# Block 2's attention with the low part of k on both halves of the partitions

## The chip, the cores and the metric

The kernel runs on one core of one Trainium2 chip. The metric is the device time of one execution in microseconds; the median of three runs is given, and the lowest and the highest beside it. A profile of one execution was recorded apart from these; all rows come from it. The engines are TensorE (PE for its matmuls, PEld for its weight loads), VectorE (DVE), ScalarE (ACT), GpSimd (POOL) and SyncE (SP, whose queue issues the loads).

## What is computed

Two blocks over 256 tokens of width 1024, all in float32. Block 1 is an attention and a gated delta rule side by side, then a mixture of 32 experts. Block 2 takes its result as the latent tokens, and 256 context tokens, modulates both, projects q (latent only), k and v, and runs two attentions beside each other, of 8 heads of 64 each, over the latent and the context keys together: type a with 2 heads of k and v, a window of 128 tokens and a sink, type b with 8 heads and a 2D neighbourhood with a bias table. Then an output projection and a gated FFN of 2816 columns follow. The part that matters, of type a; type b has its own k and v for each head and adds the bias to the local scores:

```python
def _window_gqa_latent(q, k, v, k_ctx, v_ctx, sink):
    ...
    s_loc = jnp.einsum('bnqkgd,bnjkd->bnkgqj', qb, kb).astype(jnp.float32) * scale
    s_loc = jnp.where(mask, s_loc, -jnp.inf)
    s_ctx = jnp.einsum('bnqkgd,bjkd->bnkgqj', qb, k_ctx).astype(jnp.float32) * scale
    ...
    p = jax.nn.softmax(jnp.concatenate([s_loc, s_ctx, sink_col], axis=-1), axis=-1)
```

## The kernel before

Every matrix product is made of parts. A float32 operand is split into a high part that TensorE's reduced format holds exactly (a ScalarE copy, split_w's line L185 for weights) and a low part, the rest (a subtraction on VectorE or POOL, L192). A projection or FFN product is three matmuls, high by high, low by high and high by low (mm3, recorded at the helper's line L99, as all matmuls are; transposes stand at L102).

**Scores of block 2.** A head has 64 channels, half of the 128 partitions. So q lies with its high part on one half of the partitions and its low part on the other (qa and qb, made in qk_heads, L1128 to L1153). The high part of k lies on both halves (kAa, kAb), so that one matmul over all 128 rows gives both q_high k_high and q_low k_high. The low part of k lies on one half only: kLa for type a holds the two heads of k, kLb for type b the two heads of a pair on the two halves. The product with it is a second matmul, over 64 rows, with q's high part. All four live in one tile per side, k, made by kv_tiles (L1159): for the latent it is a slot of the ring (k0, L1407), for the context it lies in the pool kvc (L1264 to L1269), where kAb has a tile of its own.

In scores (L1526) a unit is a type, a pair of heads m and a half qt of the queries; it makes eight products into two PSUM tiles (the context's first, then the latent's), adds the mask (type a, L1541) or the bias (type b, L1543) by one more matmul each, takes the maximum (L1545, VectorE), the exponential (L1555, ScalarE) and the scaling by one over the sum (L1564 ScalarE, L1566 VectorE). turn (L1569) transposes the probabilities on TensorE and copies them out, outputs (L1581) multiplies by v. There are 16 units, type a first; the loop (L1613 to L1648) puts a unit's scores one ahead of the transposes of the unit before (AHEAD = 1):

```python
                kh, kl = (kAa[s][:, m // 2], kLa[s][rs, m // 2]) if typ == 0 else (kAb[s][:, s_, m], kLb[s][rs, m])
                PE.matmul(scs[s_][:, s], lhsT=q[:, s_, m, ts], rhs=kh, start=True, stop=False)
                PE.matmul(scs[s_][:, s], lhsT=q[rs, s_, m, ts], rhs=kl, start=False, stop=s == 1)
```

**What sets the order.** A scheduler places the recorded instructions on each engine once, when the program is built; on the chip each engine takes its own in that order and waits by semaphores. Weights pass through a ring of nine tiles of 128 x 2048 (load_block, L164, ring_tile, L1165); a load is issued on SP's queue when the slot's last reader is done. During attention some ring slots are held by k0 and the bias tables; cst3 (the rotary table, the neighbourhood mask and a reversal matrix), the rotary factors rgt (rg in the trace) and the latent's v (vb0) have places in the stage's own pool.

**The FFN** (L1682 to L1748) takes 11 blocks of 256 hidden columns. Block 0's gate weights are split early (w0, L1685). mod_T (L1385) makes the transposed and modulated x in eight steps, hif (high, ScalarE) and lof (low, VectorE). g2B (L1691), the last gate spread over the rows, is laid into the place of vb0. ffn_up(b) (L1699) loads and splits gate and up weights and makes pfg and pfu, 48 products each; fsg (L1720) is the SiLU. The low part of block 0's up weights is computed on POOL.

Of the kernel before, what the change touches and what calls it, by code (L numbers as in the profile page):

```python
# [9 lines left out]
F32 = mybir.dt.float32  # L10
# [12 lines left out]
# columns of the shape-only constant array  # L23
C_ID, C_TRI = 0, 128
C_IO = 256                     # 1..32 along the free axis
C_DN = C_IO + 32               # 8..1
C_SP = C_DN + 8                # p % 32 + 1
C_BM = C_SP + 1                # [p, 4]: p // 32 == j
C_SL = C_BM + 4                # rows of a modulation chunk's partial sums: latent, context
C_LT = C_SL + 2                # [i, j] of 8 by 8: j < i  # L30
C_W = C_LT + 64
# columns of the one of block 2's attention
C_ROPE = 0                     # [p, 2 token tiles, cos 64 | signed sin 64]
C_CM = C_ROPE + 256            # [p, 64]: NEG where the column lies outside row 63 - p % 64's neighbourhood
C_J = C_CM + 64                # reversal of each half's 64 rows, times the root of the head's size
# [3 lines left out]
def constants():  # L39
    """arrays that depend on the shapes alone"""  # L40
# [31 lines left out]
    # [e, unit, slot]: e == 4 * unit + slot // 32  # L72
# [4 lines left out]
class Ordered:  # L77
    """the tensor engine; between start() and stop() it takes its instructions in the program's order"""
# [27 lines left out]
def tile_kernel(ctx: ExitStack, tc: tile.TileContext, I, out, dbg=None):  # L106
# [9 lines left out]
    def open_stage(name, psum, base=False):  # L116
        """the pools of one stage; psum: banks per tag"""
        st = ExitStack()
        if base:
            S_["base"] = st.enter_context(tc.tile_pool(name="base_" + name, bufs=1, reuse_waits="tile"))  # L120
        S_["act"] = st.enter_context(tc.tile_pool(name="act_" + name, bufs=1, reuse_waits="tile"))
        if psum:
            S_["ps"] = st.enter_context(tc.tile_pool(name="ps_" + name, bufs=1, space=PSUM, reuse_waits="tile"))
        S_["banks"] = psum
        S_["tmp"] = S_["act"]
        S_["junk"] = {"a": ("zg", 2), "c": ("jk", 1), "d": ("prb2", NPR)}[name]
        return st
# [4 lines left out]
    def open_part(name, psum):  # L132
        """pools of a part of the stage: SBUF for what only the part needs, and all of its PSUM"""
# [22 lines left out]
    # ---------------------------------------------------------------- helpers  # L156
    def load_block(src, name, extra=None):
        """src: DRAM AP [128, a, b] with a * b = 2048; extra: a pool and its slots that the stage adds to the ring"""
# [8 lines left out]
    def cols(w, c0, n=256):  # L167
        """columns c0:c0+n of a [1024, *] matrix, contraction row d = p * 8 + k"""
        return w[:, c0:c0 + n].rearrange("(p k) c -> p k c", k=8)

    def rows(w, r0):
        """rows r0:r0+256 of a [*, 1024] matrix, contraction row k * 128 + p"""
# [28 lines left out]
    def after(ins, first):  # L201
        """ins behind first in their engine's order"""
# [6 lines left out]
    def bcast_dma(dst, src, n):  # L209
        """n elements of DRAM copied to all partitions"""  # L210
        SP.dma_start(dst, bass.AP(tensor=src.tensor, offset=src.offset, ap=[[0, P], [1, n]]))

    def rstd_of(ssq, n, mean, eps, name):
        """(ssq * mean + eps) ** -0.5 over [128, n]"""
# [6 lines left out]
    def row_ssq(src, name, col=None):  # L221
        """src [128, 2, 1024] -> sums of squares [128, 2]"""
# [9 lines left out]
    def row_rstd(src, name):  # L232
        """src [128, 2, 1024] -> rstd [128, 2]"""
        return rstd_of(row_ssq(src, name), 2, 1.0 / D, EPS, name)

    def diags(r, name):
        """diagonal matrices of the two columns of r [128, 2]"""
# [5 lines left out]
    def norm_rows(src, name):  # L243
        """the rows' rstd, a column for each token tile"""
# [3 lines left out]
    def pairs_T(src, dg, tags, by_pair=False):  # L248
        """four PSUM tiles of pairs of k, [128 d, 2, 256 t]: see scaled_T"""
# [10 lines left out]
    def scaled_T(src, dg, tags, by_pair=False):  # L260
        """yields k, PSUM [128 d, 256 t] of src[t, p * 8 + k], times r[t] where dg = diags(r);
        tags: the banks of the four pairs of k, each open until its pair was taken"""
# [3 lines left out]
    # -------------------------------------------------------------- constants  # L266
# [13 lines left out]
    cols_ = const.tile([P, 4, 8], F32)    # gains down the partitions: attn_norm, ffn_norm, norm1_g, norm2_g  # L280
    gA, gF, gN1, gN2 = (cols_[:, i] for i in range(4))
    lvl = ab([P, 5, 32], "lvl", "lvl", dt=BF16)     # masks of the doubling

    mqk = ring.tile([P, 2048], F32, tag="blk", name="mqk")
    POOL.memset(mqk[:, :P], 0.0)                 # takes its slot of the ring
# [21 lines left out]
    maskn = const.tile([P, P], BF16)      # [j, i]: NEG where j > i  # L307
    maskc = const.tile([P, P], BF16)      # [i, j]: NEG where j > i

    # ============================================================ block 1: norm  # L310
# [33 lines left out]
    PE.transpose(pm, tri, ident)          # [i, j]: j <= i  # L344
# [15 lines left out]
    # ------------------------------------------------- modulations of block 2  # L360
# [4 lines left out]
    DVE.tensor_tensor(sc2t, sc2t, c2t, op=ALU.mult)                         # silu  # L365
    sil = ep.tile([P, 8, 2, 16], F32, tag="sil", name="sil")
    POOL.tensor_copy(sil, bc(sc2t.rearrange("p a k -> p k a"), 16))
    mod = pers.tile([P, 6, 8, 2], F32, tag="mod", name="mod")     # [p, vector, k, latent / context], d = p * 8 + k
    w_mod = I["w_mod_2"][0]

    def mod_steps():
        """a vector's quarters by column groups: column 8 c + k of group j is d = (32 j + c) * 8 + k, and blocks of 32
        by 32, transposed, bring its two sides to mod's places"""
# [35 lines left out]
    # ------------------------------------------------------ GDN q, k, v with conv  # L409
    gT = {}  # L410

    def proj_T(c0, name, sink):
        """columns c0:c0+256 in two [128 ch, 256 t] PSUM tiles, each given to sink with its place; a step at a time"""
# [21 lines left out]
    def gdn_proj(kind, base):  # L435
        def conv(c, pp_):
# [11 lines left out]
            DVE.scalar_tensor_tensor(o, th, 1.0, a, op0=ALU.add, op1=ALU.mult)   # 2 * silu  # L448
# [17 lines left out]
    # ------------------------------------------------------------- gates  # L466
# [17 lines left out]
    DVE.scalar_tensor_tensor(ny, y, -1.0, y, op0=ALU.mult, op1=ALU.min)     # -|y|  # L484
# [9 lines left out]
    DVE.scalar_tensor_tensor(pp, pp, 1.0, s, op0=ALU.add, op1=ALU.mult)     # log1p(z) / 2  # L494
    DVE.tensor_scalar(y, y, 0.0, None, op0=ALU.max)
    DVE.scalar_tensor_tensor(gg, pp, 2.0, y, op0=ALU.mult, op1=ALU.add)     # softplus
    DVE.scalar_tensor_tensor(gg, gg, -1.0, expA[:, None, :].to_broadcast([P, 2, 4]), op0=ALU.mult, op1=ALU.mult)
    DVE.tensor_scalar(bt, bt, 1.0, None, op0=ALU.add)
    DVE.reciprocal(bt, bt)                                                   # beta
    dump("gg", gg)  # L500
    # running sums of the log decay inside each half, and the sums after a token of the first half
    pall = aa([P, P], "kn", "pall", bufs=2)
    DVE.tensor_scalar(pall, tri, -1.0, 1.0, op0=ALU.mult, op1=ALU.add)       # [j', j]: j' > j
# [3 lines left out]
    nG = aa([P, 3, 4], "nG", "nG")        # -G0, -G1, suffix sums  # L507
# [3 lines left out]
    # ------------------------------------------------------------ gz, MoBA q, k, v  # L511
    def proj_tok(c0, name, sink):
        """columns c0:c0+256 in a [128 t, 2, 256] PSUM tile"""
# [15 lines left out]
    def projections():  # L529
        """of v, the gate and MoBA, a step at a time"""  # L530
# [64 lines left out]
    BD = []                                  # B's blocks of 32 on the diagonal, transposed  # L595
# [9 lines left out]
    # ------------------------------------- (I + B)^-1 of each half, block sizes doubling  # L605
    # up to 32: T, and its transpose W, hold the blocks on the diagonal side by side
# [32 lines left out]
    def level_32(blk):  # L639
        """pairs of blocks of 32: all of W's, the first of T's"""  # L640
# [84 lines left out]
    # the output's norm: o = c * ob with c = rq / (2 * sqrt(128))  # L725
# [30 lines left out]
    mst = at([P, 4, 3, 2, 2], "mst", "mst")          # [.., m, (max, sum, 1 / sum), head, q tile]  # L756
# [59 lines left out]
    def moba_out(m, s_, pe_, pT):  # L816
        rs = slice(64 * s_, 64 * s_ + 64)
        vs = slice((2 * m + s_) * 64, (2 * m + s_) * 64 + 64)
        # transposed blocks: (k0, q0), (k0, q1), (k1, q1)
# [32 lines left out]
    # ============================================================ block 1: experts  # L852
# [51 lines left out]
    def first_max(v, n, dn, name):  # L904
        """max over the last axis and the one-hot of its first place"""
# [19 lines left out]
    # rank of every expert in the group: those of larger logits, and those of the same logit before it  # L925
# [20 lines left out]
    rrp = at([P, 2, 32], "rrp", "rrp")              # place in the expert's list + 1, 0 where not selected  # L946
    DVE.scalar_tensor_tensor(rrp, prk, 1.0, sel, op0=ALU.add, op1=ALU.mult)
    # pairs past the 32 places of an expert, and how many there are
# [3 lines left out]
    # one-hots of the places of units 2 * g and 2 * g + 1  # L952
# [16 lines left out]
    oh = sm([P, 2, 2, 8], "oh")                     # one-hots of the first and second place  # L969
# [6 lines left out]
    # the two shares 1 / (1 + e2), e2 / (1 + e2), times the group's probability  # L976
# [18 lines left out]
    # weights and norm factors of the pairs  # L995
# [5 lines left out]
    # ------------------------------------------------------------ the experts  # L1001

    wg_, wu_, wd_ = I["w_gate"][0], I["w_up"][0], I["w_down"][0]
    # the slots of the experts' weights in the order in which they come free; None: the ring's
# [3 lines left out]
    def ring_slot():  # L1008
        """takes one of the ring's slots out of the experts' order"""
        queue.remove("r")  # L1010

    def wexp(w, u, part, name):
        """a quarter of the weights of a unit's four experts, [128, expert, 512]: two contraction rows
        p * 8 + k of a gate or up matrix; the row p * 2 + part % 2 of a down matrix, one half of its columns"""
# [23 lines left out]
    def gather(u):  # L1038
        """the rows of x of a unit, [128 d, 8 k, 128 places], times the norm's gain"""
# [20 lines left out]
    def weights(g):  # L1060
        """weight and norm of every place of units 2 * g and 2 * g + 1, one column per unit"""
# [766 lines left out]
```

## Time and profile before

| | us |
|---|---|
| median of three runs | 882.71 |
| lowest, highest | 881.35, 885.22 |
| span of the profiled execution, first to last instruction | 879.8 |
| TensorE busy | 825.3 (94%) |
| VectorE busy | 422.3 (48%) |
| ScalarE busy | 296.3 (34%) |
| POOL busy | 105.6 (12%) |

The profiled execution has no time of its own beside its span. A stretch's busy times are the sums of its instructions; on TensorE neighbours overlap, so that the distance between two starts, and not a matmul's duration, tells what one costs. PEclk is the clock granted to TensorE as a share of full speed, 2.4 GHz; 0.50 is the lower level, 1.2 GHz. A timeline's row joins instructions of one line and the same operands, xcount of them; its first time is the first one's start, its second reaches to the last one's end. In brackets stands how long the engine was idle before, and what it waited for.

### The profile page before, as it was taken

To read this page: it belongs to the slowest core of one execution; us is meant where nothing else is said; L and a number is where in the kernel's file an instruction comes from. 1 tells how busy PE (TensorE), PEld (TensorE's weight loads), DVE (VectorE), ACT (ScalarE), POOL (GpSimd) and SP (SyncE) were. 2 spreads that over 40 slices of the span, in tenths; PEclk is the share of its full clock that TensorE was granted. 3 is DMA by queue.
4 is the path that set the end of the run, shared out by engine and by line. 5 is a ranking of instruction groups with operands and counts; after the bars stand their busy time and mean duration, and the time that the engine had idled before them with its cause. 6 is when DMAs were issued, how large, how long until landed. Compare 5 with 4: busy or idle time off the path is not lost.

```text
span 879.8 us, 15327 instructions
## 1 busy us (share of the span) xinstructions
PE 825.3 (94%) x6436; PEld 667.5 (76%) x6436; DVE 422.3 (48%) x927; ACT 296.3 (34%) x523; POOL 105.6 (12%) x90
## 2 busy tenths in 40 slices
PE   9999999999789988996998997999997999999997
PEld 8887887867656645773865897667686999999996
DVE  4866454644322111323224788555664655545555
ACT  4542143433110000101004662456643444444332
POOL 3111000332000000000000577100022100000000
PEclk9999999999889999897999999589999999999999
DMA  7999787495799999999599135010271655555101
GB/s 218 353 386 391 264 296 281 133 385 171 280 386 386 387 387 387 378 382 376 208 386 333 48 53 164 1 48 2 96 239 48 202 187 187 192 191 187 54 1 48
DMA packets 123416, 200.18 MB, mean 228 GB/s; under 512 B 15481, under 2 KB 62001, under 8 KB 123345
## 3 DMA queue, kind: packets, MB, share of 16 engines
q1 hardware_dynamic: 123152, 199.08, 64.5%
q8 instruction: 51, 0.84, 0.4%
q0 software_dynamic: 192, 0.11, 0.1%
q14 instruction: 21, 0.16, 0.1%
HBM read 198.23 MB, written 1.05 MB: 226 GB/s over the span
## 4 chain that ended last, share of the span: by engine, by line
PE 47%; DVE 4%; POOL 4%; issue 3%; DMA 2%; ACT 1%; SPq 1%; DVEq 0%; POOLq 0%; ACTq 0%
PE pfg L99 7%; PE pfu L99 7%; PE pf L99 7%; PE sc L99 6%; PE pgat L99 3%; PE pgu L99 2%; PE po L99 2%; PE ptp L102 2%; POOL latl L192 2%; PE pyd L99 2%; DMA eg<-in_w_gate_dram 1%; PE ckbp L99 1%; PE pqa L99 1%; PE pqb L99 1%; POOL rq L218 1%
## 5 line engine op out<-in xcount | busy, mean ns | idle before, releaser
L99 PEld LDWEIGHTS pgat<-S,x 128*128 128x128 f32 x256 | 62.5, 335 | 3.7 <-DVE xg L1051 2.1
L99 PE MATMUL pgat<-S,x 128*128 128x128 f32 x256 | 63.0, 404 | 0.6 <-PEq L1200 0.5
L99 PE MATMUL pfu<-lof,fuh 128*128 128x256 f32 x176 | 50.2, 285 | 0.0
L99 PE MATMUL pfu<-hif,fuh 128*128 128x256 f32 x176 | 50.2, 285 | 0.0
L99 PE MATMUL pfu<-hif,ful 128*128 128x256 f32 x176 | 50.2, 285 | 0.0
L99 PE MATMUL pfg<-hif,fgl 128*128 128x256 f32 x160 | 45.3, 283 | 0.0
L99 PE MATMUL pfg<-lof,fgh 128*128 128x256 f32 x160 | 45.2, 283 | 0.0
L99 PE MATMUL pfg<-hif,fgh 128*128 128x256 f32 x160 | 45.2, 283 | 0.0
L192 DVE TENSOR_TENSOR fdl<-fd,fdh 128x512 fp32r<-128x512 f32 x44 | 27.5, 687 | 31.0 <-ACT fdh L185 31.0
L1051 DVE TENSOR_TENSOR xg<-pgat,cols__83 128x512 f32<-128x512 f32 x15 | 10.4, 692 | 63.7 <-PE pgat L99 63.7
L99 PE MATMUL pyd<-ed,hid 128*32 128x512 f32 x256 | 34.1, 664 | 3.8 <-ACT hid L1326 3.8
L1320 ACT ACTIVATE sg<-pgu,r1s 128x256 f32<-128x256 f32 x8 | 3.8, 474 | 96.7 <-PE pgu L99 73.9
L1545 DVE TENSOR_REDUCE st<-sc 128x1 f32<-128x512 f32 x32 | 21.9, 691 | 28.6 <-PE sc L99 28.3
L185 ACT ACTIVATE fdh<-fd 128x1024 fp32r<-128x1024 f32 x22 | 22.1, 1052 | 39.0 <-issue 39.0
L99 PE MATMUL pf<-fdl,fh 128*128 128x512 f32 x88 | 35.0, 398 | 0.0
L99 PE MATMUL pf<-fdh,fh 128*128 128x512 f32 x88 | 34.7, 394 | 0.0
L99 PE MATMUL pf<-fdh,fl 128*128 128x512 f32 x88 | 34.1, 393 | 0.0
L99 PEld LDWEIGHTS pfu<-hif,fuh 128*128 128x128 f32 x176 | 34.1, 194 | 0.0
L99 PEld LDWEIGHTS pfu<-hif,ful 128*128 128x128 f32 x176 | 34.1, 193 | 0.0
L99 PEld LDWEIGHTS pfu<-lof,fuh 128*128 128x128 f32 x176 | 34.0, 193 | 0.0
L185 ACT ACTIVATE fuh<-fu 128x1024 fp32r<-128x1024 f32 x22 | 22.1, 1052 | 31.2 <-issue 28.7
L99 PE MATMUL sc<-k,qa 128*128 128x256 f32 (+1 forms) x64 | 28.1, 501 | 3.7 <-DVE qa L1149 3.5
(691 smaller groups left out, 2209.6 us busy)
## 6 DMA issues: line engine op xcount, KB each, us to landing
eg<-in_w_gate_dram SPq DMA_DIRECT2D x32, 1024.0 KB, 14.1
eu<-in_w_up_dram SPq DMA_DIRECT2D x32, 1024.0 KB, 14.1
ed<-in_w_down_dram SPq DMA_DIRECT2D x32, 1024.0 KB, 14.1
wmod<-in_w_mod_dram SPq DMA_DIRECT2D x24, 1024.0 KB, 9.5
fg<-in_w_gate_dram SPq DMA_DIRECT2D x11, 1024.0 KB, 5.4
fu<-in_w_up_dram SPq DMA_DIRECT2D x11, 1024.0 KB, 5.3
fd<-in_w_down_dram SPq DMA_DIRECT2D x11, 1024.0 KB, 5.0
kv<-in_w_in_dram SPq DMA_DIRECT2D x5, 1024.0 KB, 13.9
```

What stands on the lines that cost most here:

```text
L99: return self._keep(self.engine.matmul(*args, **kwargs))
L102: return self._keep(self.engine.transpose(*args, **kwargs))
L185: S_["hi"] = ACT.activation(hf[:, s], vf[:, s], AF.Copy)
L192: i = (POOL if c in pool else DVE).tensor_tensor(lf[:, s], vf[:, s], hf[:, s], op=ALU.subtract)
L218: S_["pow"] = POOL.tensor_tensor(r, v, mhalf[:, :n], op=ALU.pow)
L1051: DVE.tensor_tensor(xg[:, ks], p, bc(gF[:, ks], P), op=ALU.mult)
L1320: ACT.activation(sg, pgu[:, 0], AF.Silu, scale=r1s[:, u:u + 1])
L1545: DVE.tensor_reduce(t_[:, 0, s_:s_ + 1], sc, axis=AX.XY, op=ALU.max)
```

## The change

qk_heads writes the low part of k by heads, as the high part, and copies it to the other half of the partitions as well: two more VectorE copies of 64 x 512 for each half of the heads and each side, eight in all. With both low parts there, every second score product reads all 128 rows of q, so that it also adds the product of the two low parts. The two kLb need twice their room: the context's is a tile of its own, the latent's takes the place of the transposed context (hcT), and the tile k is half as large, so that the latent's leaves the ring. In exchange cst3, rgt and vb0 move into one ring tile, mixed, and in the FFN g2B takes a ring slot. The core of the diff:

```diff
@@ qk_heads @@
-            lo = q[there, i, ms] if s is None else kLb[s][here, ms]
+            lo = q[there, i, ms] if s is None else kLb[s][here, i, ms]
...
                 DVE.tensor_copy(hi[there, i, ms], hi[here, i, ms])
+                DVE.tensor_copy(kLb[s][there, i, ms], kLb[s][here, i, ms])
@@ kv_tiles @@
-        k = make([P, 8, 256], f"k{s}", F32R)
-        kAa[s], kLa[s], kLb[s] = k[:, 0:2], k[:, 2:4], k[:, 4:8]
+        k = make([P, 4, 256], f"k{s}", F32R)
+        kAa[s], kLa[s] = k[:, 0:2], k[:, 2:4]
@@ the context's tiles @@
-            kAb[1] = kvc.tile([P, 2, 4, 256], F32R, tag="kAb1", name="kAb1")
+            kAb[1], kLb[1] = (kvc.tile([P, 2, 4, 256], F32R, tag=nm, name=nm) for nm in ("kAb1", "kLb1"))
@@ block 2 @@
-    cst3 = at([P, C_W3], "cst3", "cst3")
+    mixed = ring_tile("mixed", F32)
+    vb0 = mixed[:, 0:1024].rearrange("p (a b) -> p a b", a=2)
+    rgt = mixed[:, 1024:1536].rearrange("p (i t s c) -> p i t s c", i=2, t=2, s=2)
+    cst3 = mixed[:, 1536:1536 + C_W3]
     SP.dma_start(cst3, I["cst3"])
...
-    k0 = ring_tile("k0").rearrange("p (a b) -> p a b", a=8)
...
+    kLb[0] = kvc.tile([P, 2, 4, 256], F32R, tag="hcT", name="kLb0")
...
-    rgt = at([P, 2, 2, 2, 64], "rg", "rg")
@@ scores @@
-                rs = (TOP, BOT)[s_]
-                kh, kl = (kAa[s][:, m // 2], kLa[s][rs, m // 2]) if typ == 0 else (kAb[s][:, s_, m], kLb[s][rs, m])
+                kh, kl = (kAa[s][:, m // 2], kLa[s][:, m // 2]) if typ == 0 else (kAb[s][:, s_, m], kLb[s][:, s_, m])
                 PE.matmul(scs[s_][:, s], lhsT=q[:, s_, m, ts], rhs=kh, start=True, stop=False)
-                PE.matmul(scs[s_][:, s], lhsT=q[rs, s_, m, ts], rhs=kl, start=False, stop=s == 1)
+                PE.matmul(scs[s_][:, s], lhsT=q[:, s_, m, ts], rhs=kl, start=False, stop=s == 1)
@@ FFN @@
-        g2B = row_bc(mod[:, 5, :, 0], at([P, D], "vb0", "g2B"), ("mo", "sm"))
+        g2B = row_bc(mod[:, 5, :, 0], ring_tile("g2B", F32)[:, 0:D], ("mo", "sm"))
```

After the change the lines of this part stand two or three lower.

With the tiles the order moves at three places. The first is VectorE in the latent projections, where k's high part (kAb) and low part (k before, kLb now) are laid down; latl is the low part of the next weights, rqv the step that POOL's rq, and with it the normalization qn of the next heads, waits for. Before:

```order
L1153 COPY kAb_4443<-kAb_4443 64x512
L192 TENSOR_TENSOR latl<-lat,lath 128x512 x2
L1087 TENSOR_REDUCE hss<-hsq 128x8
L1153 COPY kAb_4443<-kAb_4443 64x512
L216 TENSOR_SCALAR rqv<-hss 128x8
L1151 SCALAR_TENSOR_TENSOR k_4324<-pqk,gcol,kAb_4443 64x512 x2
L1153 COPY kAb_4443<-kAb_4443 64x512
L1089 TENSOR_TENSOR qn__4796<-lqp,rq 128x512
```

and now:

```order
L1153 COPY kAb_4447<-kAb_4447 64x512
L192 TENSOR_TENSOR latl<-lat,lath 128x512
L1154 COPY kLb_4408<-kLb_4408 64x512 x2
L192 TENSOR_TENSOR latl<-lat,lath 128x512
L1087 TENSOR_REDUCE hss<-hsq 128x8
L1153 COPY kAb_4447<-kAb_4447 64x512
L1151 SCALAR_TENSOR_TENSOR kLb_4408<-pqk,gcol,kAb_4447 64x512 x2
L1153 COPY kAb_4447<-kAb_4447 64x512
L216 TENSOR_SCALAR rqv<-hss 128x8
L1154 COPY kLb_4408<-kLb_4408 64x512 x2
```

Two pairs of copies have come in, and rqv stands behind the two splits of k, where it stood ahead of them.

The second place is ScalarE at the start of the FFN, where fuh is the high part of an up block, fgh that of a gate block, and the first fsg the SiLU of block 0. Before:

```order
L228 ACTIVATE jk_6161,rfq<-x 128x1024
L185 ACTIVATE fuh<-fu 128x1024 x2
L185 ACTIVATE fgh<-fg 128x1024 x2
L1401 ACTIVATE hif<-mt,mod 128x256 x8
L1455 ACTIVATE g2B<-prb 128x4x128 x2
L1720 ACTIVATE fsg<-pfg 128x512
L185 ACTIVATE fuh<-fu 128x1024 x2
```

and now:

```order
L228 ACTIVATE jk_6169,rfq<-x 128x1024
L1404 ACTIVATE hif<-mt,mod 128x256 x8
L1458 ACTIVATE g2B<-prb 128x4x128 x2
L1722 ACTIVATE fsg<-pfg 128x512
L185 ACTIVATE fuh<-fu 128x1024 x2
L185 ACTIVATE fgh<-fg 128x1024 x2
L185 ACTIVATE fuh<-fu 128x1024 x2
```

The splits of block 0's up weights and of block 1's gate weights, which stood ahead of hif, stand behind fsg.

The third is TensorE at the same point. Before, the products with block 0's gate and up weights are woven together:

```order
L99 MATMUL pfg<-hif,fg0h 128x256
L99 MATMUL pfu<-hif,fuh 128x256
L99 MATMUL pfg<-lof,fg0h 128x256
L99 MATMUL pfg<-hif,fg0l 128x256
L99 MATMUL pfg<-hif,fg0h 128x256
L99 MATMUL pfu<-lof,fuh 128x256
L99 MATMUL pfu<-hif,ful 128x256
L99 MATMUL pfu<-hif,fuh 128x256
```

and now:

```order
L99 MATMUL pfg<-hif,fg0h 128x256
L99 MATMUL pfg<-lof,fg0h 128x256
L99 MATMUL pfg<-hif,fg0l 128x256
L99 MATMUL pfg<-hif,fg0h 128x256
L99 MATMUL pfg<-lof,fg0h 128x256
```

Only pfg stands there, 48 products of it; pfu(0) follows behind them, woven with pfg(1).

## Rows read from the trace of the kernel before

**Rows 1.** The page, part 1: span, and busy time, share and instructions of TensorE.

```profile
span 879.8 us, 15327 instructions
PE 825.3 (94%) x6436; PEld 667.5 (76%) x6436; DVE 422.3 (48%) x927; ACT 296.3 (34%) x523; POOL 105.6 (12%) x90
```

**Rows 2.** Windows: length; busy us of PE, PEld, DVE, ACT, POOL; PEclk; DMA; GB/s.

```profile
549.84:589.84 40.00, 39.87 (x171) 25.84 (x171) 22.77 (x60) 19.98 (x50) 2.43 (x3) 0.66 0.00 1
589.84:638.04 48.20, 47.80 (x305) 33.78 (x306) 28.60 (x71) 30.40 (x64) 0.71 (x1) 1.00 0.20 66
549.84:576.70 26.86, 26.73 (x82) 16.81 (x82) 14.47 (x38) 12.22 (x31) 2.43 (x3) 0.50 0.00 1
600.00:610.00 10.00, 9.60 (x75) 7.42 (x74) 4.23 (x11) 4.67 (x8) 0.00 (x0) 1.00 0.01 2
```

**Rows 3.** Timeline, PE, type a (start, us, instruction, idle before): half clock, then full.

```profile
549.84 2.11 PE L99 MATMUL sc<-k,qa 128*128 128x256 f32 x4 [3.54 <-DVE qa L1149]
551.88 0.29 PE L99 MATMUL sc<-maskc,identb 128*128 128x128 bf16 x1
...
581.86 1.31 PE L99 MATMUL sc<-k,qa 128*128 128x256 f32 x4
583.10 0.23 PE L99 MATMUL sc<-maskc,identb 128*128 128x128 bf16 x1
```

**Rows 4.** Timeline, PE, one head of type b.

```profile
590.25 0.36 PE L99 MATMUL sc<-kAb,qb 128*128 128x256 f32 x1
...
591.48 0.70 PE L99 MATMUL sc<-bias,cst 128*128 128x256 f32 x2
```

**Rows 5.** Timeline, PE, two heads near 578 us, and narrow windows inside them.

```profile
577.29 2.04 PE L99 MATMUL sc<-k,qa 128*128 128x256 f32 x8
...
577.90 0.51 PE L99 MATMUL sc<-k,qa 128*128 128x256 f32 x2
...
578.33 0.38 PE L99 MATMUL sc<-k,qa 64*128 64x256 f32 x2
```

**Rows 6.** Timeline, PE, FFN: two neighbours at full clock, two at half.

```profile
697.70 0.28 PE L99 MATMUL pfg<-lof,fgh 128*128 128x256 f32 x1
697.82 0.29 PE L99 MATMUL pfg<-hif,fgl 128*128 128x256 f32 x1
...
686.16 0.42 PE L99 MATMUL pfu<-hif,ful 128*128 128x256 f32 x1
686.38 0.42 PE L99 MATMUL pfu<-hif,fuh 128*128 128x256 f32 x1
```

**Rows 7.** Timeline, DVE, latent projections.

```profile
522.93 0.43 DVE L1153 CAST kAb<-kAb 64x512 fp32r<-64x512 f32 x1
...
529.31 0.69 DVE L1089 TENSOR_TENSOR qn__4872<-lqp,rq 128x512 f32<-128x512 f32 x1 [1.75 <-POOL rq L218]
...
549.10 1.41 DVE L1149 TENSOR_TENSOR qa<-pqk,qa 64x512 fp32r<-64x512 f32 x2
```

**Rows 8.** Timelines of PE, ACT, POOL and DVE at the start of the FFN.

```profile
684.04 0.39 PE L99 MATMUL pfg<-lof,fg0h 128*128 128x256 f32 x1 [1.14 <-DVE lof L1402]
...
703.34 0.28 PE L99 MATMUL pfu<-hif,fuh 128*128 128x256 f32 x1
...
689.40 2.23 ACT L1455 ACTIVATE g2B<-prb 128x512 f32<-128x512 f32 x2
694.66 0.60 ACT L1720 ACTIVATE fsg<-pfg 128x512 f32<-128x512 f32 x1 [3.02 <-PE pfg L99]
697.80 2.01 ACT L185 ACTIVATE fuh<-fu 128x1024 fp32r<-128x1024 f32 x2 [2.54 <-PE pfu L99]
...
679.97 5.16 POOL L192 TENSOR_TENSOR ful<-fu,fuh 128x512 fp32r<-128x512 f32 x4
...
682.44 2.96 DVE L1402 SCALAR_TENSOR_TENSOR lof<-mt,mod,hif 128x256 fp32r<-128x256 f32 x2
685.73 0.47 DVE L1402 SCALAR_TENSOR_TENSOR lof<-mt,mod,hif 128x256 fp32r<-128x256 f32 x1
```

More of the change, by code (lines that the diff above doesn't have):

```diff
@@ L1406, in tile_kernel @@
         kvw[c0] = load_block(cols(w_in2, c0), "lat")
-    k0 = ring_tile("k0").rearrange("p (a b) -> p a b", a=8)
-    hth, htl = mod_T(xf, [ss[:, 4, i:i + 1] for i in range(2)], mod[:, 1], mod[:, 0], "l", lambda: kv_tiles(0, lambda shape, nm, dt: k0 if nm == "k0" else at(shape, nm, nm, dt=dt)))
+    hth, htl = mod_T(xf, [ss[:, 4, i:i + 1] for i in range(2)], mod[:, 1], mod[:, 0], "l",
+                     lambda: kv_tiles(0, lambda shape, nm, dt: vb0 if nm == "vb0" else at(shape, nm, nm, dt=dt)))
     S_["cxt"] = "tr"
     next(ctxh)
+    kLb[0] = kvc.tile([P, 2, 4, 256], F32R, tag="hcT", name="kLb0")
     if CXB:
```

## The prediction

> **What bounds the kernel now.** I read the page first, then windows over block 2's attention, then TensorE's timeline inside it, then the two places that the change also moves: the latent projections on VectorE and the start of the FFN. TensorE is busy for 94% of the 879.8 us span [rows 1], and the windows say that attention is no exception: from the first score product at 549.84 to the end of the last at 638.04 the engine has work all the time, 39.87 of 40.00 us in the heads of type a and 47.80 of 48.20 us in those of type b, while VectorE works 22.77 and 28.60 us and ScalarE 19.98 and 30.40 us [rows 2]. So what leaves TensorE here leaves the path, until VectorE is met. The granted clock stands at half (the lower level, 1.2 GHz) from the start until about 576.7 us [rows 2]; before it fell, TensorE had waited 3.54 us for the last split of q [rows 3].
>
> Busy does not mean dense. In type b one head's four products, high and low, context and latent, begin at 590.25 and its bias product at 591.48: 1.23 us, 0.31 us a product [rows 4]. In the FFN products of 256 columns over 128 rows begin 0.12 us apart at full clock and 0.21 at half [rows 6]. In type a four products take 2.04 us at half clock and 1.24 at full [rows 3]. The span of this execution is 2.9 us under the median of the three runs, 882.71; I add that at the end.
>
> **The products.** Before, every second product of a head is over 64 rows, and each neighbour is over 128. The change keeps their number, 128, their columns and very nearly their order, and gives all of them 128 rows. What will such a product cost? The nearest in form is the FFN's, 0.12 us, hundreds in a row. Inside attention there is one place where the order puts two 128-row products side by side: the second's end makes the pair 0.51 us long where one takes 0.38 to 0.39, and by their own lengths they begin 0.12 to 0.22 us apart, not 0.31 [rows 5]. So the dear step is the change between the two heights. I take 0.12 (0.21 at half clock), since after the change the whole group is of one form as in the FFN, and keep 0.22 as the dear end.
>
> - Type b, 16 heads at full clock: 1.23 - 4 x 0.12 = 0.75 us each, 12.0.
> - Type a, four heads at full clock: 1.24 - 0.48 = 0.76 each, 3.0; two heads, placed with two equal products side by side, took 1.98 us together (8 products, 2.04 to the end of the last's tail) [rows 5]; they give back 1.0.
> - Type a, ten heads at half clock: 2.04 - 4 x 0.21 = 1.20 each, 12.0.
>
> That is 28.0. Could more come off, because the clock returns sooner with denser work? In type a hardly: 40.0 - (12.0 + 3.0 + 1.0) = 24.0 us are left for TensorE, and VectorE has 22.8 us of work in it [rows 2], so at most 1.2 more, 29.2 in all. That nearness also costs. A head passes from TensorE to VectorE (the maximum), ScalarE (the exponential), back for the transposes and on; only one unit is scored ahead. Before, the slow products of 32 heads covered these turns, with 4% idle in the worst ten microseconds [rows 2]; 4% of the 60 us that remain is 2.4, which I take off: **25.6 gained**. At the dear price of 0.22 the heads give 16 x 0.35 + 4 x 0.36 + 10 x (2.04 - 4 x 0.4) and the two nothing, 11.4, the poor end.
>
> A page speaks against the change here. The Trainium skill, TensorE: Matmul & The Clock Gate, "Why this matters for your kernels", says that one product with few contraction rows takes as long as one with 128, and that products in different row groups run side by side, so that small ones are best kept small and laid in different groups. The trace bears out the second half: two 64-row products, one of each half, stand in one 0.38 us entry [rows 5]. By the first half the time between products would not come from the height, nothing would be gained, and the sum would be that of the third rival below; the 0.31 against 0.12 of rows 4 and 6 is why I go by the trace.
>
> **The copies.** qk_heads now also copies the low part of k to the other half: eight more VectorE instructions of 64x512. The nearest row is the high part's copy, 0.43 us [rows 7]. Four are the context's and stand in the expert stage, long before; VectorE is busy for 48% of the span [rows 1], and I count them as hidden in its idle time there; if that cover were gone they would cost 1.7. Four are the latent's and stand some 25 us before the first score, in the VectorE chain whose end, the split qa at 549.10 [rows 7], releases it: 1.72 us at most in themselves. That chain has waits for POOL's powers, such as 1.75 us [rows 7], and a copy that falls into one is free; the order puts one pair behind the step that POOL waits for. One step of that kind (rqv) also moves behind a split, which could add a turn on POOL of about the same size, so the ends are 0 and 3.4; I take **0.9 lost**. The half-clock stretch begins after this wait as before.
>
> **The start of the FFN.** The second block of weights, fu(0), now gets the ring slot that attention's high part of the latent k held, and its split on ScalarE stands behind fsg, which needs all 48 products pfg(0). TensorE therefore has no pfu(0) to weave in and all of pfg(0) goes first. Before, TensorE reaches the first pfu(1) at 703.34, with 144 products behind it; it waited for lof, 1.14 us at one place [rows 8]. After: g2B ends at 689.40 + 2.23 = 691.63, by when the 48 products are through; fsg adds 0.60; the first half of fuh, 1.0 (half of 2.01) [rows 8], is there at 693.2. The 96 products left take 96 x 0.12 = 11.5: 704.7. POOL's ful follows fuh by 5.16 / 4 = 1.29 [rows 8], in which products are missing: 706.0, 2.7 later than before. TensorE's idle time of some 2 us would let the clock fall, and the last such stretch, 15 products at 0.21, cost 1.4. On the other side ful is gone from the time of lof, which took 1.48 us each beside it and 0.47 alone [rows 8]: up to 2.0 back. Between 0.7 (lof earlier, no clock loss) and 7.5 (ful now slows the four splits fgl by the same 1 us each and the clock falls) I take **3.0 lost**. What is late next is fgh(1), two splits behind fuh on ScalarE.
>
> **Moves without a price.** cst3, the rotary table and the latent v share one ring tile, and its load goes ahead of three weight loads on SP's queue; those are delayed by one small load, and each is used 10 us or more after it lands. g2B's ring slot and fu(0)'s are free well before their use, as attention ends over 40 us earlier; if that cover went, the load would show as a DMA wait ahead of fuh.
>
> **The sum.** -25.6 + 0.9 + 3.0 = -21.7: a span of 858.1, and with the 2.9 of the median **861.0 us**. Good end: -29.2 + 0 + 0.7 = -28.5, 854; poor end of the one price: -11.4 + 3.4 + 7.5 = -0.5, which needs all three at once.
>
> **Rivals.** First, the chain VectorE, ScalarE, TensorE becomes the bound in attention. For it: 22.8 of VectorE's us against 24.0 left on TensorE in type a, and one unit of lead only; against it: in type b the rest, 48.2 - 12.0 = 36.2, stays 6 us above ScalarE. If type a gives 7 instead of 16 and type b 6 instead of 12, or if products come 0.22 apart, some 13 are gained: -13 + 4 = -9, 873.7. Second, the clock stays at half until the end of attention, because shorter products leave more waits. The page's clock row came back at 576.7 with the old, thinner work, which is against it. Type b's 36.2 us would take about 1.65 times that (2.04 to 1.24 for the same products [rows 3]), 60 instead of 48: -16 + 12 + 4 = 0, 882.7. Third, the other side: the height of a product does not set its time, the 0.31 us comes from the operands of the attention (weights new for each product). Then the copies and the FFN's start are all that is left: 1.7 + 4.2 = +5.9, 888.6; it decides as soon as attention gains less than the copies and the FFN's start cost. By the page named above this is how it would come out; rows 5, with equal neighbours inside attention closer than unequal ones, is against it.
>
> **Chances.** Forecast 0.76, first rival 0.15, second 0.04, third 0.05. The range must leave out no more than 2 in 10: it reaches from 853, the good end with a little for the clock, to 873, which takes in half of the first rival. Half a per cent, 4.4 us, is about what can be told from no change: the forecast and the first rival are faster, 0.91; the second is the same, 0.04; the third slower, 0.05.
>
> **What would show it.** In the profile after: all score products 128*128 and 0.12 apart, a head's four in 0.48 (right) or still 1.23 (third rival); attention 62 to 64 us long, TensorE under 100% busy in type a with VectorE above 85%; the half clock over before half of type a has passed, and none in type b; first scores 0 to 2 us later in relation to the projections; on ScalarE fsg before the first fuh, with a hole on TensorE between pfg(0) and pfu(0) of about 2 us, and the first pfu(1) some 24 us after the first pfg instead of 20.9. The prediction is wrong if TensorE's idle time in attention is above 10 us, or if the FFN's start costs more than 8.

## The result and the profile after

The changed kernel takes 858.26 us (median of four runs, 857.41 to 859.44) beside 882.39 before (four runs, one more than the three above): a ratio of 0.9724, 95% interval 0.9703 to 0.9744. All ratios below are to the kernel before, measured beside it, with their 95% intervals. The forecast was 861.0, in a range of 853 to 873. The span fell from 879.8 to 856.1 us; part 1 of the page after:

```profile
span 856.1 us, 15332 instructions
PE 796.8 (93%) x6436; PEld 656.8 (77%) x6436; DVE 425.2 (50%) x935; ACT 294.4 (34%) x523; POOL 106.7 (12%) x90
```

TensorE makes as many instructions as in [rows 1] and is busy 28.5 us less; VectorE has eight more, the copies. TensorE's timeline after, one head of type b, stands against [rows 4]:

```profile
574.62 0.39 PE L99 MATMUL sc<-kAb,qb 128*128 128x256 f32 x1
574.85 0.28 PE L99 MATMUL sc<-kLb,qb 128*128 128x256 f32 x1
574.97 0.28 PE L99 MATMUL sc<-kAb,qb 128*128 128x256 f32 x1
575.08 0.28 PE L99 MATMUL sc<-kLb,qb 128*128 128x256 f32 x1
575.20 0.59 PE L99 MATMUL sc<-bias,mixed 128*128 128x256 f32 x2
```

All four products read 128 rows. The first step is 0.23 us, the others 0.12: 0.58 from the first product to the bias, where it was 1.23. Type a, first and later, stands against [rows 3]:

```profile
551.29 1.22 PE L99 MATMUL sc<-k,qa 128*128 128x256 f32 x4 [3.55 <-DVE qa L1149]
552.32 0.33 PE L99 MATMUL sc<-maskc,identb 128*128 128x128 bf16 x1
...
557.77 0.74 PE L99 MATMUL sc<-k,qa 128*128 128x256 f32 x4 [1.10 <-ACT prb L1557]
...
562.34 0.72 PE L99 MATMUL sc<-k,qa 128*128 128x256 f32 x4
562.90 0.23 PE L99 MATMUL sc<-maskc,identb 128*128 128x128 bf16 x1
```

Four products take 1.03 us at half clock (551.29 to 552.32) and 0.56 at full. The wait for qa ahead of the first is as long as before, and a new kind of wait appears, for the exponential prb. The windows (type a, type b, the stretch at half clock) stand against [rows 2]:

```profile
551.29:574.62 23.33, 21.44 (x174) 18.97 (x174) 21.44 (x60) 17.60 (x47) 2.46 (x3) 0.87 0.02 4
574.62:610.36 35.74, 35.34 (x303) 29.50 (x300) 28.41 (x71) 30.13 (x65) 0.71 (x1) 1.00 0.17 59
551.29:557.40 6.11, 5.38 (x24) 4.82 (x24) 4.90 (x9) 1.64 (x3) 2.46 (x3) 0.50 0.00 0
```

The 88.2 us of attention have become 59.1, from 551.29 to 610.36. In type a TensorE and VectorE are now equally busy, 21.44 of 23.33 us each, and TensorE has 1.9 us of idle time; the clock is back at 557.4 instead of 576.7. The latent projections stand against [rows 7]; VectorE's timeline shows the new copies, which a trace calls casts:

```profile
520.41 0.88 DVE L1154 CAST kLb<-kLb 64x512 fp32r<-64x512 f32 x2
...
526.19 0.87 DVE L1154 CAST kLb<-kLb 64x512 fp32r<-64x512 f32 x2
...
550.55 1.41 DVE L1149 TENSOR_TENSOR qa<-pqk,qa 64x512 fp32r<-64x512 f32 x2
```

0.44 us each, as taken. And the start of the FFN (PE, then ACT, POOL, DVE), against [rows 8]:

```profile
655.01 0.38 PE L99 MATMUL pfg<-hif,fg0h 128*128 128x256 f32 x1
...
663.67 0.28 PE L99 MATMUL pfg<-hif,fg0l 128*128 128x256 f32 x1
665.58 0.39 PE L99 MATMUL pfu<-hif,fuh 128*128 128x256 f32 x1 [1.63 <-ACT fuh L185]
...
666.93 0.58 PE L99 MATMUL pfu<-hif,ful 128*128 128x256 f32 x1 [0.85 <-POOL ful L192]
...
679.65 0.28 PE L99 MATMUL pfu<-hif,fuh 128*128 128x256 f32 x1
...
663.98 0.60 ACT L1722 ACTIVATE fsg<-pfg 128x512 f32<-128x512 f32 x1 [1.94 <-PE pfg L99]
664.47 2.00 ACT L185 ACTIVATE fuh<-fu 128x1024 fp32r<-128x1024 f32 x2
...
665.60 5.92 POOL L192 TENSOR_TENSOR ful<-fu,fuh 128x512 fp32r<-128x512 f32 x4 [13.26 <-ACT fuh L185]
...
667.44 5.22 DVE L192 TENSOR_TENSOR fgl<-fg,fgh 128x512 fp32r<-128x512 f32 x4 [6.93 <-ACT fgh L185]
```

TensorE finishes pfg(0), waits 1.63 us for fuh, which stands behind fsg, and 0.85 for ful; the first pfu(1) comes at 679.65, 24.6 us after the first pfg, where it came 20.9 us after it. Beside each other, POOL's ful and VectorE's fgl take 1.48 and 1.3 us each. Before, ful took 1.29 [rows 8] and fgl 0.62:

```profile
689.93 2.49 DVE L192 TENSOR_TENSOR fgl<-fg,fgh 128x512 fp32r<-128x512 f32 x4
```

The balance of the two profiles:

| | before | after | difference |
|---|---|---|---|
| first score product | 549.84 | 551.29 | +1.45 |
| first score to the end of the last | 88.20 | 59.07 | -29.13 |
| from there to the first pfg | 44.36 | 44.65 | +0.29 |
| first pfg to first pfu(1) | 20.94 | 24.64 | +3.70 |
| rest | 176.5 | 176.5 | 0.0 |
| span | 879.8 | 856.1 | -23.7 |

Not all of the first line is the copies': a step of the expert stage ahead of the first copy, va of the context, begins at 384.35 before and at 385.00 after. That 0.65 is one execution against another; in the profiles below the first score comes between 549.9 and 555.4 us, with copies and without, and stages are compared from their own starts.

### The profile page after: what moved, and what is told of

It reads as the page before. It is cut to its first block, busy times and chain, and to the rows that moved or that the text cites. A ratio compares the mean times of both kernels' runs of the same rounds, so it can differ in the third digit from the quotient of the medians.

```text
span 856.1 us, 15332 instructions
## 1 busy us (share of the span) xinstructions
PE 796.8 (93%) x6436; PEld 656.8 (77%) x6436; DVE 425.2 (50%) x935; ACT 294.4 (34%) x523; POOL 106.7 (12%) x90
## 4 chain that ended last, share of the span: by engine, by line
PE 45%; DVE 7%; POOL 3%; ACT 2%; issue 2%; DMA 1%; SPq 0%; DVEq 0%; POOLq 0%; ACTq 0%
PE pfu L99 8%; PE pfg L99 7%; PE pf L99 7%; PE sc L99 3%; PE pgat L99 3%; PE pgu L99 3%; PE po L99 2%; PE ptp L102 2%; PE pyd L99 2%; PE ckbp L99 2%; PE pqa L99 1%; PE pqb L99 1%; POOL latl L192 1%; DMA sinkB<-in_sink_a_dram 1%; PE pt L99 1%
## 5 line engine op out<-in xcount | busy, mean ns | idle before, releaser
L185 ACT ACTIVATE fdh<-fd 128x1024 fp32r<-128x1024 f32 x22 | 22.1, 1052 | 36.9 <-issue 36.9
L185 ACT ACTIVATE fuh<-fu 128x1024 fp32r<-128x1024 f32 x22 | 22.1, 1053 | 36.4 <-issue 28.6
L192 DVE TENSOR_TENSOR fgl<-fg,fgh 128x512 fp32r<-128x512 f32 x40 | 27.7, 754 | 9.3 <-ACT fgh L185 9.3
L99 PE MATMUL pgu<-eg,xg 128*32 128x256 f32 x512 | 31.5, 387 | 0.0
```

The lines of the kernel that those rows point to most:

```text
L99: return self._keep(self.engine.matmul(*args, **kwargs))
L185: S_["hi"] = ACT.activation(hf[:, s], vf[:, s], AF.Copy)
L192: i = (POOL if c in pool else DVE).tensor_tensor(lf[:, s], vf[:, s], hf[:, s], op=ALU.subtract)
```

## The experiments

The theory: a product costs 0.12 us where its neighbour has the same number of rows, and some 0.19 more where it has not; the rest of the change only costs. The rivals: the 64-row product is dear by itself; the gain is the clock's; the moved tiles gain something.

**Products back to 64 rows (e_half).**

```diff
-                kh, kl = (kAa[s][:, m // 2], kLa[s][:, m // 2]) if typ == 0 else (kAb[s][:, s_, m], kLb[s][:, s_, m])
+                rs = (TOP, BOT)[s_]
+                kh, kl = (kAa[s][:, m // 2], kLa[s][rs, m // 2]) if typ == 0 else (kAb[s][:, s_, m], kLb[s][rs, s_, m])
...
-                PE.matmul(scs[s_][:, s], lhsT=q[:, s_, m, ts], rhs=kl, start=False, stop=s == 1)
+                PE.matmul(scs[s_][:, s], lhsT=q[rs, s_, m, ts], rhs=kl, start=False, stop=s == 1)
```

> The change with the second product of every head put back to 64 rows; copies, tiles and the FFN's order stay as in the change. My theory (a change of height between neighbouring products costs time, the rest of the change only costs): attention as long as before, 88 us from the first score product to the end of the last, products 0.31 us apart in type b, half clock again for some 27 us; the copies' 0.8 us and the FFN start's 3.7 us remain, so 882.4 + 4.5 = 887 us. Rival (the gain comes from the new places of the tiles, not from the products): 858 to 865. Rival (copies and FFN start cost nothing that counts): 882.

Measured: 899.42 us (888.36 to 902.14), ratio 1.0138 (1.0087 to 1.0189), slower than before by 1 to 2%, and 12 us above the 887 expected. The 0.31 us spacing is back:

```profile
597.71 0.36 PE L99 MATMUL sc<-kAb,qb 128*128 128x256 f32 x1
598.00 0.38 PE L99 MATMUL sc<-kLb,qb 64*128 64x256 f32 x1
598.31 0.39 PE L99 MATMUL sc<-kAb,qb 128*128 128x256 f32 x1
```

So the tiles and copies gain nothing. Nine of the ten runs fall into two groups, three around 888.5 (near the 887 expected) and six around 900, with mean granted clocks of 0.953 to 0.955 and 0.937 to 0.945. The profiled run, 893.3, lies between: its clock is 0.955, and its first score comes at 555.44, 5.6 us later than before, of which the copies explain less than 1; its attention, 90.0 us, is 1.8 longer. No run of the upper group was profiled; the next two experiments show what can make such a difference.

**One type alone (e_typa, e_typb).** For type a the low part of k lies on both halves in the kernel before too: kLa holds each of its two heads twice, and one head of a pair reads the upper half, the other the lower (rs in the loop). The description of the kernel before, with the low part on one half only, holds for type b alone. So e_typa needs neither copies nor moved tiles; the kernel before gets, in the loop of scores:

```diff
-                kh, kl = (kAa[s][:, m // 2], kLa[s][rs, m // 2]) if typ == 0 else (kAb[s][:, s_, m], kLb[s][rs, m])
+                kh, kl = (kAa[s][:, m // 2], kLa[s][:, m // 2]) if typ == 0 else (kAb[s][:, s_, m], kLb[s][rs, m])
+                ql = q[:, s_, m, ts] if typ == 0 else q[rs, s_, m, ts]
...
-                PE.matmul(scs[s_][:, s], lhsT=q[rs, s_, m, ts], rhs=kl, start=False, stop=s == 1)
+                PE.matmul(scs[s_][:, s], lhsT=ql, rhs=kl, start=False, stop=s == 1)
```

> The kernel before, with 128 rows for type a alone; its low part of k already lies on both halves, so there are no copies, no moved tiles and the FFN starts as before. My theory: type a falls from 40.4 to about 23.3 us, 17 gained, the half clock lasts 6 us, type b stays at 48: 865 us. Rival (the clock comes back by itself after some 27 us, whatever TensorE does): type a falls by 12 at most, and the half clock reaches into type b, 870 to 875.

e_typb is the mirror image, the changed kernel with 64 rows for type a.

> The change with 64 rows for type a's second products, 128 for type b. My theory: type a 40 us as before with the half clock for 27 us, type b 35.7 instead of 47.8 (12 gained), 0.8 and 3.7 lost for copies and FFN start: 875 us. Rival (the gains of the two types are not independent, most of it hangs on the clock): above 880.

Measured: e_typa 864.7 us, ratio 0.9778 (0.9705 to 0.9852), as the theory has it. e_typb 885.69 us (876.14 to 887.58), ratio 0.9983 (0.9935 to 1.0032), no different from before: three of ten runs at 876 to 877, where the theory put it, seven at 885 to 888, on the rival's side of 880. The windows of type a and type b of e_typa, and then of e_typb, from one of its longer runs:

```profile
549.97:572.06 22.09, 20.23 (x174) 18.17 (x175) 21.46 (x59) 17.91 (x49) 2.46 (x3) 0.93 0.04 5
572.06:619.90 47.84, 47.44 (x303) 33.23 (x303) 28.94 (x72) 30.96 (x68) 0.71 (x1) 1.00 0.19 65
```

```profile
551.98:602.66 50.68, 50.53 (x174) 33.34 (x175) 24.01 (x64) 20.07 (x50) 2.47 (x3) 0.50 0.01 2
602.66:639.38 36.72, 36.32 (x302) 30.36 (x300) 27.08 (x67) 29.21 (x61) 0.71 (x1) 0.96 0.16 57
```

Type b's 36 us come with 128 rows (36.7 here, its first 2.9 at half clock; 35.7 in the change) and its 47.8 us with 64, whatever type a does. Type a is another matter: with alternating rows its length depends on how long the half clock lasts. Here it lasted for all of type a, 50.7 us, and a little beyond, though TensorE was busy throughout; in the profile of before it lasted 27 us, in e_half's 30.7. With rows of one number it lasted 3.4 us in e_typa and 6.8 after. That 10 us of difference in type a (50.7 against 40.4) is as large as the distance between e_typb's two groups of runs, and their mean granted clocks point the same way: 0.954 to 0.959 in the three shorter runs, 0.940 to 0.944 in the seven longer. No shorter run was profiled. So the change also takes away a risk: its nine runs, of two sets, stay at 861.3 us or below, while the kernel before, at 882.5 as a rule, had three of nineteen runs beside these at 888 to 894. The rivals on the clock are wrong in one form, since the clock did not come back by itself after some fixed time, and right in another: part of the gain is the clock's, and in e_typa, where only type a's products changed, it came back after 3.4 us.

**The FFN's start (e_g2b, g2b_r).**

```diff
-        g2B = row_bc(mod[:, 5, :, 0], ring_tile("g2B", F32)[:, 0:D], ("mo", "sm"))
+        g2B = row_bc(mod[:, 5, :, 0], mixed[:, 0:D], ("mo", "sm"))
```

> The change, with g2B laid into the tile mixed, in the place of the latent's v, in place of a ring slot of its own; by the order fu(0) is split ahead of hif again and pfg(0) and pfu(0) are woven as before. My theory (the FFN's start costs 3.7 us because of the slot that g2B takes): 858.3 - 3.7 = 854.6 us, the first pfu(1) about 21 us after the first pfg. Rival (what the late split costs is given back, since lof is no longer slowed): 857 to 859.

Measured: 854.26 us, ratio to before 0.9660 (0.9587 to 0.9732). ScalarE takes fuh ahead of hif again:

```profile
651.30 1.99 ACT L185 ACTIVATE fuh<-fu 128x1024 fp32r<-128x1024 f32 x2
...
655.76 1.31 ACT L1404 ACTIVATE hif<-mt,mod 128x256 fp32r<-128x256 f32 x3 [0.58 <-DVE mt L1403]
```

```profile
656.32 0.39 PE L99 MATMUL pfg<-hif,fg0h 128*128 128x256 f32 x1
...
676.03 0.28 PE L99 MATMUL pfu<-hif,fuh 128*128 128x256 f32 x1
```

The first pfu(1) comes 19.7 us after the first pfg: the slot that g2B takes is what delayed the FFN. In a later set of runs, beside the change itself:

> The change again, beside the next two on one chip, as their measure. All theories: 858 to 859 us, half clock for 7 to 10 us.

> The change with g2B in the tile mixed, again, to set the gain against the change on one chip. My theory: 4 us faster than the change, 854 to 855 us.

The change took 857.76 there (0.9715, 0.9688 to 0.9742) and this version 856.6 (852.89 to 859.32; 0.9676, 0.9649 to 0.9704), so its lead in the medians was 1.2 us, not 4, and the intervals of this pair overlap. At the start of the FFN this version's profile kept the gain:

```profile
660.15 0.39 PE L99 MATMUL pfg<-hif,fg0h 128*128 128x256 f32 x1
...
681.08 0.28 PE L99 MATMUL pfu<-hif,fuh 128*128 128x256 f32 x1
```

That is 20.9 us, against 24.6 in the change's profile of this set: 3.7 us again. It lost elsewhere. Its first score came 4.2 us later (555.05 against 550.86), a delay that stands ahead of block 2's first context product already (391.85 against 387.69) and so ahead of everything that the edit moves; and it had the half clock for 13.7 us of type a, which took 25.0 instead of 23.4. So the slot costs 3.7 to 4.9 us at the start of the FFN in both pairs of profiles, while the lead of the whole kernel, 1 to 4 us, also hangs on stages ahead that differ from run to run by as much.

**64 rows, but grouped (e_group2, e_group4, e_win2, e_win4).** This tells a dear product from a dear change between products. The kernel before, with two (e_group2) or four (e_group4) products of each height in a row. In these kernels and the next ones the grouped order is also fixed on TensorE (by PE.on, in lines not shown), where the scheduler is otherwise free to change it. The core of e_group4:

```diff
+        for lows in range(2):
+            for s in (1, 0):
+                for s_ in range(2):
...
+                    if lows == 0:
+                        PE.matmul(scs[s_][:, s], lhsT=q[:, s_, m, ts], rhs=kh, start=s == 1, stop=False)
+                    else:
+                        PE.matmul(scs[s_][:, s], lhsT=q[rs, s_, m, ts], rhs=kl, start=False, stop=False)
```

> The kernel before with the products of a unit grouped by height, still 64 rows for the low part: for each side two of 128 rows, then two of 64 (one of each half), so 4 changes of height per unit in place of 8. My theory (a change costs about 0.19 us, equal neighbours stand 0.12 apart): a unit's eight products take 8 x 0.12 + 4 x 0.19 = 1.7 us instead of 2.46 in type b, or 1.5 if the two 64-row products run side by side; 6 to 8 us gained in type b, 6 to 9 in type a: 866 to 871 us. Rival (a 64-row product is dear by itself, some 0.5 us wherever it stands): 882, no change.

> As the last, with four of 128 rows and then four of 64: 2 changes of height per unit (the second side's first product no longer starts its bank, which the first side's has started). My theory: 8 x 0.12 + 2 x 0.19 = 1.34 us a unit in type b, 1.1 if pairs of 64-row products run side by side; 9 to 11 us gained in type b, 13 to 16 in type a: 856 to 860 us. Rival (64 rows dear by themselves): 882.

Measured: 865.9 us, ratio 0.9813 (0.9797 to 0.9830), and 860.09, 0.9750 (0.9734 to 0.9767), each at an edge of what was expected, with the products, rows and copies of before. A unit of e_group4 on TensorE:

```profile
593.95 0.79 PE L99 MATMUL sc<-kAb,qb 128*128 128x256 f32 x4
594.66 0.50 PE L99 MATMUL sc<-k,qb 64*128 64x256 f32 x4
595.09 1.13 PE L99 MATMUL sc<-bias,cst 128*128 128x256 f32 x4
```

Eight products in 1.14 us, where the kernel before took 2.46, e_group2 takes 1.36 and the change 2 x 0.58. The four 64-row products together last 0.50, hardly more than one (0.38): two of one half and two of the other run side by side. The rival of the dear 64-row product is out; what costs is the change of height, and grouped, four products of 64 rows are the cheaper ones: 0.43 us from the first of them to the bias product, against 0.58 for the change's four.

e_win2 and e_win4 put type a at 128 rows and keep the grouping.

> The kernel before with type a at 128 rows and type b grouped by two as in e_group2; no copies, no moved tiles. My theory: 17 gained in type a, 6 to 8 in type b, nothing lost: 857 to 859 us. Rival (64 rows dear by themselves): 865, as type a alone.

> The kernel before with type a at 128 rows and type b grouped by four as in e_group4; no copies, no moved tiles. My theory: 17 gained in type a, 9 to 11 in type b, nothing lost: 854 to 857 us, faster than the change without its copies. Rival: 865, as type a alone.

Measured: 862.5 us (0.9768, 0.9747 to 0.9789) and 859.24 (0.9748, 0.9726 to 0.9770), 3.5 and 2.2 us above the ranges expected. Type b lasted 37.5 us in e_win4, 10.3 less than before, as expected, but type a 28.0 instead of e_typa's 22.1. These kernels also forced both heads' products of type a into groups, which is not needed there and makes the first head's maximum wait for the second head's products; the half clock lasted 10.2 us in two stretches. How much is due to each was not separated.

**Type a in its own order, type b grouped (e_mix).** The loop of scores, from the kernel before:

```diff
+        for lows in ((0,), (1,)) if typ else ((0, 1),):
...
+                        if typ == 0:
+                            PE.matmul(scs[s_][:, s], lhsT=q[:, s_, m, ts], rhs=(kAa, kLa)[low][s][:, m // 2], start=low == 0, stop=low == 1 and s == 1)
+                        elif low == 0:
+                            PE.matmul(scs[s_][:, s], lhsT=q[:, s_, m, ts], rhs=kAb[s][:, s_, m], start=s == 1, stop=False)
+                        else:
+                            PE.matmul(scs[s_][:, s], lhsT=q[rs, s_, m, ts], rhs=kLb[s][rs, m], start=False, stop=False)
```

> The kernel before with type a at 128 rows in the old order of its products, and type b at 64 rows grouped by four (64-row pairs side by side); no copies, no moved tiles. My theory: 17 to 18 gained in type a (22 us left, as in the run of type a alone), 9 to 10 in type b (37 to 38 left, as in the runs grouped by four), nothing lost: 854 to 856 us, as fast as the change with g2B in mixed. Rival (the grouping in type b was slowed by the same waits that made type a 28 us in the grouped runs, and 128 rows are needed for the rest): 858 to 860.

Measured: 853.02 us (851.56 to 854.04), ratio 0.9642 (0.9618 to 0.9666), the lowest of all; on the same chip the change took 857.76, and the two intervals do not overlap. Against e_g2b and g2b_r, whose intervals overlap with this one, the order is open. Windows of type a and type b:

```profile
552.97:576.10 23.13, 21.24 (x175) 19.02 (x175) 21.56 (x59) 17.95 (x49) 2.48 (x3) 0.87 0.02 4
576.10:613.93 37.83, 37.83 (x325) 30.64 (x325) 28.33 (x74) 31.87 (x69) 1.08 (x1) 1.00 0.25 83
```

Type a is as in the change and type b 2.1 us longer, with 22 more of TensorE's instructions in its window (325 against 303), outputs and transposes that the change has behind its last score. The FFN starts in the order of before, and the copies, the second kLb and the moved tiles are not needed.

## Why the prediction was right

**The products.** The step taken from the FFN's rows held: 0.12 us between products of one form, 0.56 to 0.58 for a head's four with the first step counted, where 0.48 was put. Type b, forecast at 12.0, gave 12.05 at full clock on both sides: 47.79 from its first score product at 590.25 to 638.04 before, 35.74 now. e_group4 shows that the reason was the right one: the change of height, and not the height. The Trainium skill, TensorEngine Tiling (Array Packing), "Key Properties", says that changing the tiling mode drains TensorE; the runs agree that a change costs time, 0.31 us against 0.12, and no trace here shows the draining as such. The rule weighed in the prediction (the Trainium skill, TensorE: Matmul & The Clock Gate, "Why this matters for your kernels") was half right: the 64-row products do run side by side, and leaving them at 64 rows costs next to nothing once they are grouped (1.14 us a unit against 1.16). Read alone it would have kept the alternation.

**The clock.** This term was mis-sized. "In type a hardly: at most 1.2 more" held VectorE's work in the stretch at 22.8 us; with the stretch shorter, 21.44 fell into it. Type a, from its first score to type b's, gave 40.41 - 23.33 = 17.1 us with its 1.9 us of waits already off, where 16.0 was forecast with none off, so that attention gained 29.1 and not 25.6 and fell to 59.1 us, below the 62 to 64 named as a sign. Beyond that, I had priced ten heads at the half clock of one profile as if its length were a property of the kernel. e_typb shows the same alternating type a at 50.7 us, e_half at 42.3: a length of 27 us was one outcome among several.

**The waits.** 2.4 was taken off for turns that shorter products no longer cover; TensorE was idle for 1.9 us in type a and 0.4 in type b, where it had been 0.1 and 0.4: 1.8 more, all of it in type a. The first rival, a chain through VectorE and ScalarE as the bound, came near in type a, where VectorE is busy 92% of the time, but not in type b.

**The copies.** 0.9 forecast. Ahead of kn in the projections the profile after is 0.85 late (505.31 to 504.46), of which 0.65 was there before any copy; from there to the first score it loses 0.60 more. So 0.8 for all eight, 0.2 of it the context's that I had called hidden. The latent's 0.6 is firm: from the first latent product with b's k (lkbp) to the first score it is 60.7 us in all seven profiles without copies and 61.3 in all six with them. The context's 0.2 is less than one execution differs from another ahead of lkbp: from the context's first product with b's k (ckbp) to there the thirteen profiles take 100.7 to 102.6 us.

**The FFN's start.** 3.0 forecast, a choice between 0.7 and 7.5 and no sum, and 3.7 measured, by the steps named: fsg ends 9.6 us after the first pfg (9.8 forecast), the first half of fuh is there at 10.5 (10.8), the holes for fuh and ful are 1.63 and 0.85, and POOL's ful and VectorE's fgl slow each other, which I had only at the dear end. The fall of the clock, feared there for 1.4, made no difference: a half-clock stretch of 3.4 us lies in this part both before and after. e_g2b removed all of the loss by taking away the slot, and with it the only part of the change that lost anything of size; its other 1.2 us (19.7 against 20.9) go with a half-clock stretch that fell ahead of the first pfg.

**The sum.** -21.7 forecast, -23.7 in the profile: 3.5 more gained in attention, and against it 0.7 more lost at the FFN, 0.3 in the output projection that no term had, and the 0.65 of the expert stage. The median was forecast 2.7 too high, the last 0.7 of it because 2.9 was added to the span where 2.2 was found. The mechanism was right; that the sum came so near is in part luck, since these misses have opposite signs. The third rival's sum takes 4.2 for the start of the FFN where the forecast takes 3.0, without a reason; it decides nothing.

## What to carry to other kernels

Read the distance between the starts of neighbouring matmuls, not how busy TensorE is: alternating products of 64 and 128 contraction rows cost 0.31 us each where like neighbours cost 0.12. Before spending memory and copies to give all of them one height, try the order: grouped by height, the small ones in pairs on both halves, the same products were as fast and nothing else had to move. Before copying an operand, look also at where it lies already: type a, with 17 of the 29 us, needed no copy, only other rows in one matmul call. And check who inherits a slot when a tile enters a ring: here 3.7 us went to one split that came behind the SiLU instead of ahead of it.

## What was not expected

The length of a half-clock stretch varies from run to run and follows the kind of work in it. After the same 3.5 us wait ahead of type a, the clock was at half for 3.4 to 13.7 us in the profiles with type a's products of one height (eight profiles, five of them at 6.8 or less; in e_win2 and e_win4 two stretches together), for 17.1 us in both with 64-row products grouped there, and for 27 to 55 us in the three with alternating ones, where the trace calls TensorE busy for over 99% of the time from the first score on. The stretches from the first score on in e_group4, e_half and e_typb:

```profile
549.95:566.50 16.55, 15.05 (x65) 10.90 (x66) 12.83 (x33) 10.54 (x27) 2.44 (x3) 0.50 0.01 1
555.44:586.00 30.56, 30.44 (x93) 19.28 (x93) 15.45 (x40) 13.27 (x33) 2.44 (x3) 0.50 0.00 1
551.98:605.50 53.52, 53.37 (x188) 35.53 (x190) 24.90 (x67) 22.04 (x55) 2.47 (x3) 0.50 0.05 20
```

A profile's one stretch is a sample, and where a kernel's runs fall into groups, as e_typb's at 876 and 886 us, this is a place to look.

What holds the clock down in the alternating stretch is not shown beyond that; whether a like number of products with more idle time between them would do the same was not tried.
